# Another order of the columns inside the TensorE matmuls of a short-convolution block

## The chip, the cores and the metric

The kernel runs on one core of one Trainium2 chip. The metric is the device time of one execution in microseconds (us), from runs of the whole program. A profile is one execution recorded by the hardware profiler, and its span runs from the first to the last instruction on the core.

## The reference

With `DEPTH = 1` the reference has one layer, the gated short convolution; the SSD mixer is in the file and isn't reached. `x` has 1024 rows of 1024 numbers, all float32:

```python
def short_conv_mixer(u, w_in, conv_w, w_out):
    z, bg, cg, v = jnp.split(u @ w_in.astype(u.dtype), 4, axis=-1)   # w_in: 1024 x 8192
    y = bg * causal_dwconv(cg * v, conv_w) * jax.nn.silu(z)          # conv_w: 3 x 2048
    return y @ w_out.astype(u.dtype)                                 # w_out: 2048 x 1024

u = rms_norm(x, pre_norm)
out = x + rms_norm(short_conv_mixer(u, w_in, conv_w, w_out), post_norm)
```

Nearly all of the work is in the two matrix products: 1024 x 1024 by 1024 x 8192, then 1024 x 2048 by 2048 x 1024.

## The kernel before

**The products.** Each of the two products is cut into 2 x 2 blocks and done by a scheme with seven block products in place of eight, named a to g; from pair 4 on some of the seven (b, then f, then g) are cut a second time in the same way, into a' to g'. A number is kept as the sum of two parts, hi and lo, of type float32r, and a product is three matmuls: lo by hi, hi by lo, hi by hi. A matmul here multiplies a stationary tile of 128 x 128 (weights, loaded by an instruction of its own that the profile calls LDWEIGHTS) by a moving tile of 128 rows, and adds the result to a tile of PSUM, one bank of 512 float32 a partition. A product of the first level moves 512 columns, a product of the second level 256.

**Five functions issue these matmuls.** `product` (line 865) does the blocks a to g of the input product, 12 matmuls of 512 columns each; `plain` (1117) does the first pair of column blocks, 512 columns, without the scheme of seven; `deep_product` (1460) does a' to g', 6 matmuls of 256 columns each; `out_mm` (1887) does a, c, d, e and g of the output product, 512 columns; `small_mm` (1980) does its b and f, 256 columns. In every one the moving operand and the PSUM tile are walked from the first column to the last. The moving operand is a part of one of the `u` tiles in SBUF (four blocks of 512 columns for hi, four for lo), or of a smaller tile of the second level (`ub..`, `uf..`, `ug.._deep`). The stationary operands are pages of 512 columns (`wah`, `dwb0l` and so on), of which a matmul takes 128.

**Order of the work.** From `plan.record()` on, no instruction is issued at once: `Plan.call` (line 290) writes down each one with the operands it reads and writes, an estimate of its duration, and what it needs. For a view of a tile it takes the lowest and the highest element number, and the count of elements (lines 302 to 330); a matmul is estimated at `n / 2400 + 0.0135` us for `n` elements a partition. `Plan.arrange` (428) then orders the instructions of VectorE, ScalarE, GpSimd and of the DMA queues by due times that come from the order of the matmuls, which is fixed by the list `slots` (1676), and `Plan.emit` (658) issues them. Views are objects of the class `View`, whose `rearrange` keeps both the element numbers and the step to be repeated on the real operand.

**Around the products.** ScalarE copies a page to its hi part, VectorE subtracts to get the lo part, GpSimd builds the sums of blocks that the scheme of seven needs, VectorE and ScalarE take finished banks out of PSUM, and VectorE does the convolution. SBUF places are chosen by hand: tables of page numbers (`HEAD_SLOTS`, line 24; `LOW_PAGES`, 209), of `u` tiles (`U_LAYOUT`, 205), and unused stretches of 64 and 416 bytes between pools. By these tables every matmul operand starts at a multiple of 64 bytes in its partition.

Of the kernel before, what the change touches and what calls it, by code (L numbers as in the profile page):

```python
# [668 lines left out]
def kernel(  # L669
# [16 lines left out]
    nc = plan = Plan(tc.nc)  # L686
# [6 lines left out]
    HB = 512  # L693
# [22 lines left out]
    def bank(name):  # L716
        return psum.tile([P, HB], F32, tag="bank", name=name)
# [136 lines left out]
    UH, UL = {}, {}  # L854
# [7 lines left out]

    banks = {}

    def product(p, i, ks=None):

        w = wt[p, i]
        which = {"b": "y", "e": "v", "f": "v"}.get(i, "x")
        first = i in "abe"
        if first and (p, which) not in banks:  # L870
            banks[p, which] = bank(f"p{which}_{p}")
        ps = banks[p, which]
        for k in range(KH) if ks is None else ks:
            hi, lo = (h[:, k * P : (k + 1) * P] for h in w)
            last = k == KH - 1
            nc.tensor.matmul(ps, lo, UH[i][:, k], start=first and k == 0, stop=False, skip_group_check=True)
            nc.tensor.matmul(ps, hi, UL[i][:, k], start=False, stop=False, skip_group_check=True)
            nc.tensor.matmul(ps, hi, UH[i][:, k], start=False, stop=last, skip_group_check=True)

    sn, cvs = {}, {}  # L880

# [235 lines left out]
    def plain(p, n, half, part, kks=range(4), first=None, last=None):  # L1117

        i = "abef"[2 * half + part]
        if (p, n, half) not in banks:  # L1120
            banks[p, n, half] = bank(f"pp_{p}_{n}_{half}")
        ps, w = banks[p, n, half], plain_w[p, n, part]
        first = part == 0 if first is None else first
        last = part == 1 if last is None else last
        for j, kk in enumerate(kks):
            hi, lo = (h[:, kk * P : (kk + 1) * P] for h in w)
            end = last and j == len(kks) - 1
            nc.tensor.matmul(ps, hi, UH[i][:, kk], start=first and j == 0, stop=False, skip_group_check=True)
            nc.tensor.matmul(ps, lo, UH[i][:, kk], start=False, stop=False, skip_group_check=True)
            nc.tensor.matmul(ps, hi, UL[i][:, kk], start=False, stop=end, skip_group_check=True)  # L1130

    def plain_snap(p, n):
        t = page(f"sp{n}_{p}")
# [69 lines left out]
    for k in range(KH):  # L1203
        plain(0, 0, 0, 0, [k], first=k == 0)
        for t in range(TH - 2 if k < KH - 1 else 0, TH):
            turn(k + KH, t)
# [5 lines left out]
    square_v(TH + 1)  # L1212
    plain_snap(0, 0)
    plain(0, 1, 0, 0)
    for k in (6, 7):
        read_k(k)
    high_plain(0, 1, [1])
    low_plain(0, 1, [1])
    plain_snap(0, 1)
    plain(0, 0, 0, 1)  # L1220
    plain(0, 1, 0, 1)
    rebuild([0])
# [45 lines left out]
    def plain_late(kk, part):  # L1268

        for n in (0, 1):  # L1270
            plain(0, n, 1, part, [kk], first=part == 1 and kk == 0, last=part == 0 and kk == KH - 1)

    product(1, "b", (0, 1))
    turn2(0)
    second(0)
    product(1, "b", (2, 3))
    sn[1, "a"] = page("sna_1")
    nc.scalar.copy(sn[1, "a"], banks[1, "y"])
    product(1, "a", (0, 1))
    turn2(1)  # L1280
    second(1)
# [105 lines left out]
    HH, KQ = HB // 2, KH // 2  # L1387
# [72 lines left out]
    def deep_product(z, c, i):  # L1460


        n, off = DEEP_W[i]
        if z == "f" and i in ("b'", "g'"):
            ps, first = banks[2 * c + (i == "g'"), "v"], False
        elif z == "g" and i in ("b'", "f'", "g'"):
            ps, first = banks[2 * c + (i == "g'"), "x"][:, HH if i == "f'" else 0 :], False
        else:
            which, first = z + DEEP_C[i][0], i in ("a'", "b'", "e'")
            if first:  # L1470
                banks[c, which] = bank(f"p{which[1]}2{z}_{c}")
            ps = banks[c, which]
        ps = ps[:, :HH]
        for k in range(KQ):
            hi, lo = (h[:, off + k * P : off + (k + 1) * P] for h in deep_w[z, c, n])
            if (z, i) in deep:
                uh, ul = (t[:, k] for t in deep[z, i])
            else:
                kk, l0 = {"a'": (k, 0), "b'": (k + KQ, 0), "e'": (k, HH), "f'": (k + KQ, HH)}[i]
                uh, ul = (u[z][:, kk, l0 : l0 + HH] for u in (UH, UL))  # L1480
            nc.tensor.matmul(ps, lo, uh, start=first and k == 0, stop=False, skip_group_check=True)
            nc.tensor.matmul(ps, hi, ul, start=False, stop=False, skip_group_check=True)
            nc.tensor.matmul(ps, hi, uh, start=False, stop=k == KQ - 1, skip_group_check=True)

    def deep_after(c, i):
        which, row, half = DEEP_C[i]
# [190 lines left out]
    for p in range(2, len(PAIRS)):  # L1677
        q, c = p + 1, p // 2
# [91 lines left out]
    for n, slot in enumerate(slots):  # L1770
        if slot[2:]:
            z, i, c = slot
# [24 lines left out]
        i, p = slot  # L1797
# [89 lines left out]
    def out_mm(i, h, q):  # L1887
        which = "v" if i == "e" else "x"
        if (which, q) not in ob:
            ob[which, q] = bank(f"po_{which}{q}")  # L1890
        ps, u, y = ob[which, q], OP["u", i, h], OP["y", i, h]
        for k in range(CQ):
            hi, lo = (y[:, z, k, q * P : (q + 1) * P] for z in (0, 1))
            first, last = i in "abe" and h == 0 and k == 0, h == 1 and k == CQ - 1
            nc.tensor.matmul(ps, lo, u[:, 0, k], start=first, stop=False, skip_group_check=True)
            nc.tensor.matmul(ps, hi, u[:, 1, k], start=False, stop=False, skip_group_check=True)
            nc.tensor.matmul(ps, hi, u[:, 0, k], start=False, stop=last, skip_group_check=True)

    def halves_of(t):
        q = t % TH  # L1900
# [79 lines left out]
    def small_mm(of_, i):  # L1980
        which = {"b'": "y'", "e'": "v'", "f'": "v'"}.get(i, "x'")
        first = i in ("a'", "b'", "e'")
        if first:
            ob[which] = bank(f"p{of_}_{which[0]}")
        if i in OUT_A:
            n, a0 = OUT_A[i]
            yh, yl = (small_op[of_, n][:, z, :, a0 : a0 + HH] for z in (0, 1))
        else:
            yh, yl = (small_op[of_, "X"][:, 0, z] for z in (0, 1))
        if i in OUT_B:  # L1990
            n, b0 = OUT_B[i]
            uh, ul = (small_op[of_, n][:, z, :, b0 : b0 + HH] for z in (0, 1))
        else:
            uh, ul = (small_op[of_, "X"][:, 1, z] for z in (0, 1))
        for j in (0, 1):
            ps = ob[which][:, j * HH : (j + 1) * HH]
            for k in range(CQ):
                hi, lo = (y[:, k, j * P : (j + 1) * P] for y in (yh, yl))

                start, stop = first and j == 0 and k == 0, k == CQ - 1  # L2000
                nc.tensor.matmul(ps, lo, uh[:, k], start=start, stop=False, skip_group_check=True)
                nc.tensor.matmul(ps, hi, ul[:, k], start=False, stop=False, skip_group_check=True)
                nc.tensor.matmul(ps, hi, uh[:, k], start=False, stop=stop, skip_group_check=True)

    def small_add(of_, i):
        which, row, half = DEEP_C[i]
# [5 lines left out]
    def product_b():  # L2012
        for i in SMALL:
            small_mm("b", i)
            small_add("b", i)
            if i == "b'":
                sums_y("b", "f", nc.vector)
                split_small("b", "X")
            elif i in ("e'", "d'", "f'", "g'"):
                split_unit()  # L2020
                fetch_unit()
            if i in ("f'", "g'"):
                for q in (0, 1) if i == "f'" else (2, 3):
                    early_half(q)

    def product_f():
        split_small("f", "B3")
        load_res(0)
        load_res(1)
        for i in SMALL:  # L2030
            small_mm("f", i)
            small_add("f", i)
            if i == "b'":
                split_small("f", "X")
            elif i in ("e'", "d'", "f'", "g'"):
                split_unit()
                if i != "e'":
                    fetch_unit()
            if i in ("f'", "g'"):
                for q in (0, 1) if i == "f'" else (2, 3):  # L2040
                    norm_square(q, 1)
# [33 lines left out]
    for i, h in OUT[:-2]:  # L2075
        if i in "bf":
            if h == 0:
                product_b() if i == "b" else product_f()
            continue
        for q in range(TH):  # L2080
            out_mm(i, h, q)
        BESIDE[i, h]()
        if h == 1:
            for q in range(TH):
                combine(i, q)
# [5 lines left out]
    for q in range(TH):  # L2091
        for h in (0, 1):
            out_mm("g", h, q)
        if q == TH - 1:
            plan.flush(PLAN)
        combine("g", q)
        finish_row(q + TH)
# [24 lines left out]
```

## Time and profile before

| | |
|---|---|
| time, median of 3 runs | 770.9 us (770.83 to 771.6) |
| span of the profiled execution | 768.7 us |
| the profiled execution's own time | not given apart from its span; the median stands 2.2 us above the span |
| matmuls on TensorE | 4320 records: 2244 of 512 columns, 1974 of 256, 102 small ones |
| TensorE busy with matmuls | 758.4 us, 99% |
| VectorE, GpSimd, ScalarE busy | 678.9, 464.1 and 459.4 us |

The counts of 512 and 256 columns follow from the code: a to g and the first pair give 2244, the second level 42 for each of 14 + 13 + 12 blocks and 168 for each of the two small output products, 1974 in all.

How to read the views: all instructions of the kernel carry line 292, the helper that issues them, so they are told apart by tile names. PE is the matmul row of TensorE, PEld its weight loads, DVE is VectorE, ACT ScalarE, POOL GpSimd. In a group's row `px<-u_a,wah` is output, moving operand, weights; the two numbers at the end are busy time and the mean duration of one. Matmuls are pipelined, so a duration is longer than the distance from one start to the next; the chain of waits gives that distance, since each of its pieces runs from the first start of a group to the first start of the next, with the count of instructions behind it.

### The profile page before, as it was taken

The page shows a single profiled execution, that of the slowest core. Times are in us where ns is not written, and L with a number is a line of the kernel's source. Part 1 is how long each engine was busy: PE and PEld are TensorE (multiplying, and loading weights), DVE is VectorE, ACT ScalarE, POOL GpSimd, SP SyncE. Part 2 cuts the span into 40 slices and gives each one's busy share as a digit, 9 for nine tenths or more (in the row PEclk, how much of TensorE's full clock was granted, in tenths as well). Part 3 has the DMA queues.
Part 4 walks back from the last instruction along what each step waited for, and adds up shares of the span by engine and source line. Part 5 has one row for each costly group of instructions (what it writes and reads, how often), then busy time and mean ns, then how long its engine had stood idle before and what let it go on. Part 6 is the DMA issues. An engine that isn't in the chain of part 4 may idle for free.

```text
span 768.7 us, 12791 instructions
## 1 busy us (share of the span) xinstructions
PE 758.4 (99%) x4320; PEld 665.9 (87%) x4320; DVE 678.9 (88%) x1022; ACT 459.4 (60%) x880; POOL 464.1 (60%) x416
## 2 busy tenths in 40 slices
PE   8999999999999999999999999999999999999996
PEld 6888888898989898988898898989888889889885
DVE  6899978999988979989999999898988898877993
ACT  7765678675656565556555665556553656564731
POOL 2509997889675778696789678584739100600421
PEclk9999999999999999999999999999999999999999
DMA  9213325243333547576859484928465998666842
GB/s 317 68 55 84 110 83 150 103 139 130 98 117 97 171 110 200 136 187 164 252 125 255 103 240 97 255 85 211 122 177 179 334 363 291 203 221 204 278 148 109
DMA packets 117137, 130.11 MB, mean 169 GB/s; under 512 B 7320, under 2 KB 74704, under 8 KB 116944
## 3 DMA queue, kind: packets, MB, share of 16 engines
q1 hardware_dynamic: 112560, 120.77, 49.3%
q0 software_dynamic: 4352, 8.39, 7.2%
q8 instruction: 34, 0.56, 0.3%
q14 instruction: 31, 0.25, 0.1%
q10 hardware_dynamic: 160, 0.14, 0.1%
HBM read 101.74 MB, written 44.30 MB: 190 GB/s over the span
## 4 chain that ended last, share of the span: by engine, by line
PE 97%; DVE 1%; DMA 1%; ACT 0%; POOL 0%; issue 0%; POOLq 0%; ACTq 0%
PE px L292 39%; PE pv L292 15%; PE po_x L292 11%; PE px2b L292 5%; PE px2f L292 4%; PE px2g L292 3%; PE po_v L292 3%; PE pp L292 3%; PE pv2b L292 3%; PE pv2f L292 2%; PE pf_x L292 1%; PE pb_x L292 1%; PE py2b L292 1%; PE py L292 1%; PE pv2g L292 1%; PE pb_v L292 1%
## 5 line engine op out<-in xcount | busy, mean ns | idle before, releaser
L292 PE MATMUL px<-u_a,wah 128*128 128x512 f32 x248 | 76.6, 390 | 0.0
L292 PE MATMUL px<-u_c,wch 128*128 128x512 f32 x248 | 76.5, 390 | 0.0
L292 PE MATMUL px<-u_d,wdh 128*128 128x512 f32 x248 | 76.4, 389 | 0.0
L292 PE MATMUL pv<-u_e,weh 128*128 128x512 f32 x248 | 76.3, 389 | 0.0
L292 ACT COPY beside<-raw 128x512 f32<-128x512 f32 x67 | 39.6, 591 | 31.1 <-DVE wal L292 10.4
L292 DVE SCALAR_TENSOR_TENSOR cv<-gpad,cw,cv 128x1024 f32<-128x1024 f32 x32 | 51.6, 1612 | 3.5 <-ACT cv L292 3.3
L292 PEld LDWEIGHTS px<-u_c,wch 128*128 128x128 f32 x248 | 46.5, 188 | 8.9
L292 PEld LDWEIGHTS px<-u_a,wah 128*128 128x128 f32 x248 | 46.6, 188 | 8.9
L292 PEld LDWEIGHTS pv<-u_e,weh 128*128 128x128 f32 x248 | 46.5, 188 | 8.7
L292 PEld LDWEIGHTS px<-u_d,wdh 128*128 128x128 f32 x248 | 46.6, 188 | 8.6
L292 POOL TENSOR_TENSOR sf<-raw,sc 128x512 f32<-128x512 f32 x30 | 47.2, 1573 | 9.5 <-DVE sc L292 7.1
L292 PE MATMUL px<-u_a,wal 128*128 128x512 f32 x124 | 48.4, 391 | 0.0
L292 PE MATMUL px<-u_c,wcl 128*128 128x512 f32 x124 | 48.4, 391 | 0.0
L292 PE MATMUL px<-u_d,wdl 128*128 128x512 f32 x124 | 48.4, 390 | 0.0
L292 PE MATMUL pv<-u_e,wel 128*128 128x512 f32 x124 | 48.2, 389 | 0.0
L292 POOL TENSOR_TENSOR rs_post<-ve_post,minus_half 128x1 f32<-128x1 f32 x7 | 6.5, 941 | 67.3 <-DVE ve_post L292 67.3
L292 POOL TENSOR_TENSOR sc<-se,raw 128x512 f32<-128x512 f32 x25 | 35.0, 1401 | 19.2 <-DVE se L292 10.2
L292 POOL TENSOR_TENSOR raw<-raw,raw 128x512 f32<-128x512 f32 x31 | 44.6, 1437 | 3.2 <-DVE se L292 2.9
L292 ACT COPY sna<-px 128x512 f32<-128x512 f32 x30 | 17.6, 586 | 45.4 <-PE px L292 45.1
L292 POOL TENSOR_TENSOR se<-raw,raw 128x512 f32<-128x512 f32 x22 | 32.8, 1491 | 18.1 <-DMA raw<-in_sc_w_in 11.3
L292 DVE TENSOR_TENSOR wcl<-sc,wch 128x512 fp32r<-128x512 f32 x31 | 31.7, 1023 | 2.8 <-ACT wch L292 2.8
L292 DVE TENSOR_TENSOR sna<-px2b,sna 128x256 f32<-128x256 f32 x56 | 23.2, 415 | 10.2 <-PE px2b L292 10.2
(486 smaller groups left out, 2637.3 us busy)
## 6 DMA issues: line engine op xcount, KB each, us to landing
raw<-in_sc_w_in SPq DMA_DIRECT2D x128, 256.0 KB, 4.7
y_d<-cv SPq DMA_DIRECT2D x16, 512.0 KB, 2.9
s_d<-s SPq DMA_DIRECT2D x32, 256.0 KB, 4.9
t_d<-in_sc_w_out POOLq DMA_DIRECT2D x16, 512.0 KB, 8.5
tb<-in_sc_w_out SPq DMA_DIRECT2D x16, 256.0 KB, 3.5
t_d<-in_sc_w_out SPq DMA_DIRECT2D x16, 256.0 KB, 4.6
t_d<-t_d SPq DMA_DIRECT2D x16, 256.0 KB, 4.5
s<-y_d SPq DMA_DIRECT2D x16, 256.0 KB, 4.6
```

Source lines behind the costliest of these rows:

```text
L292: getattr(engine, name)(*(self.plain(a) for a in args), **{k: self.plain(a) for k, a in kw.items()})
```

## The change

A function `walk` is added, and the output and the moving operand of every matmul of the five functions go through it. It changes the order in which the columns of the operand are read and the columns of the bank are written; the two are changed in the same way, so that each column of the result lands where it did. With 512 columns the order is columns 0 to 3, 16 to 19, 32 to 35 and so on to 496 to 499; then 4 to 7, 20 to 23 and so on; four such passes of 32 pieces. A piece is 16 bytes and the next one starts 64 bytes behind it. With 256 columns it is 0 to 63, 128 to 191, 64 to 127, 192 to 255: four pieces of 256 bytes. The stationary operand, the number of instructions, the tiles and their places are as before. The matmuls of `stir` and the transposes (`turn`) don't go through `walk`.

```diff
     banks = {}
 
+    def walk(a):
+        if a.shape[-1] == HB:
+            return a.rearrange("p (h c n) -> p c h n", c=4, n=4)
+        return a.rearrange("p (h c n) -> p c h n", h=2, n=64)
+
     def product(p, i, ks=None):
...
-            nc.tensor.matmul(ps, lo, UH[i][:, k], start=first and k == 0, stop=False, skip_group_check=True)
-            nc.tensor.matmul(ps, hi, UL[i][:, k], start=False, stop=False, skip_group_check=True)
-            nc.tensor.matmul(ps, hi, UH[i][:, k], start=False, stop=last, skip_group_check=True)
+            nc.tensor.matmul(walk(ps), lo, walk(UH[i][:, k]), start=first and k == 0, stop=False, skip_group_check=True)
+            nc.tensor.matmul(walk(ps), hi, walk(UL[i][:, k]), start=False, stop=False, skip_group_check=True)
+            nc.tensor.matmul(walk(ps), hi, walk(UH[i][:, k]), start=False, stop=last, skip_group_check=True)
...
# deep_product; plain, out_mm and small_mm are changed in the same way
-            nc.tensor.matmul(ps, lo, uh, start=first and k == 0, stop=False, skip_group_check=True)
-            nc.tensor.matmul(ps, hi, ul, start=False, stop=False, skip_group_check=True)
-            nc.tensor.matmul(ps, hi, uh, start=False, stop=k == KQ - 1, skip_group_check=True)
+            nc.tensor.matmul(walk(ps), lo, walk(uh), start=first and k == 0, stop=False, skip_group_check=True)
+            nc.tensor.matmul(walk(ps), hi, walk(ul), start=False, stop=False, skip_group_check=True)
+            nc.tensor.matmul(walk(ps), hi, walk(uh), start=False, stop=k == KQ - 1, skip_group_check=True)
```

More of the change, by code (lines that the diff above doesn't have):

```diff
@@ L1127, in plain @@
             end = last and j == len(kks) - 1
-            nc.tensor.matmul(ps, hi, UH[i][:, kk], start=first and j == 0, stop=False, skip_group_check=True)
-            nc.tensor.matmul(ps, lo, UH[i][:, kk], start=False, stop=False, skip_group_check=True)
-            nc.tensor.matmul(ps, hi, UL[i][:, kk], start=False, stop=end, skip_group_check=True)
+            nc.tensor.matmul(walk(ps), hi, walk(UH[i][:, kk]), start=first and j == 0, stop=False, skip_group_check=True)
+            nc.tensor.matmul(walk(ps), lo, walk(UH[i][:, kk]), start=False, stop=False, skip_group_check=True)
+            nc.tensor.matmul(walk(ps), hi, walk(UL[i][:, kk]), start=False, stop=end, skip_group_check=True)
     def plain_snap(p, n):
@@ L1894, in out_mm @@
             first, last = i in "abe" and h == 0 and k == 0, h == 1 and k == CQ - 1
-            nc.tensor.matmul(ps, lo, u[:, 0, k], start=first, stop=False, skip_group_check=True)
-            nc.tensor.matmul(ps, hi, u[:, 1, k], start=False, stop=False, skip_group_check=True)
-            nc.tensor.matmul(ps, hi, u[:, 0, k], start=False, stop=last, skip_group_check=True)
+            nc.tensor.matmul(walk(ps), lo, walk(u[:, 0, k]), start=first, stop=False, skip_group_check=True)
+            nc.tensor.matmul(walk(ps), hi, walk(u[:, 1, k]), start=False, stop=False, skip_group_check=True)
+            nc.tensor.matmul(walk(ps), hi, walk(u[:, 0, k]), start=False, stop=last, skip_group_check=True)
     def halves_of(t):
@@ L2000, in small_mm @@
                 start, stop = first and j == 0 and k == 0, k == CQ - 1
-                nc.tensor.matmul(ps, lo, uh[:, k], start=start, stop=False, skip_group_check=True)
-                nc.tensor.matmul(ps, hi, ul[:, k], start=False, stop=False, skip_group_check=True)
-                nc.tensor.matmul(ps, hi, uh[:, k], start=False, stop=stop, skip_group_check=True)
+                nc.tensor.matmul(walk(ps), lo, walk(uh[:, k]), start=start, stop=False, skip_group_check=True)
+                nc.tensor.matmul(walk(ps), hi, walk(ul[:, k]), start=False, stop=False, skip_group_check=True)
+                nc.tensor.matmul(walk(ps), hi, walk(uh[:, k]), start=False, stop=stop, skip_group_check=True)
     def small_add(of_, i):
```

## The prediction

> **What bounds the kernel now.** I read the page's busy times and the chain that ended last first.
>
> ```profile
> span 768.7 us, 12791 instructions
> PE 758.4 (99%) x4320; PEld 665.9 (87%) x4320; DVE 678.9 (88%) x1022; ACT 459.4 (60%) x880; POOL 464.1 (60%) x416
> PEclk9999999999999999999999999999999999999999
> PE 97%; DVE 1%; DMA 1%; ACT 0%; POOL 0%; issue 0%; POOLq 0%; ACTq 0%
> ```
>
> TensorE fills 99% of the span and 97% of the chain, and its granted clock is full throughout. A busy PE is not yet a PE at its peak, so the next view is the list of its own waits.
>
> ```profile
> PE pk L292 <- DVE ve_pre L292: 1.5, 1, 1.5
> PE pw L292 <- DVE idle L292: 1.1, 1, 1.1
> PE pp L292 <- ACT u_a L292: 0.5, 1, 0.5
> PE pk L292 <- DVE xa L292: 0.4, 1, 0.4
> ```
>
> That is 3.5 us in all, in the head. The matmuls follow each other, and the time is their count by the distance from one start to the next. The chain in order of time gives that distance (start, us until the next piece, tile, count). First the middle of the input product, then the output product:
>
> ```profile
> 303.14 2.72 PE pv L292 x12
> 305.86 0.71 PE pv2b L292 x6
> 306.57 0.71 PE pv2f L292 x6
> 307.27 0.71 PE px2b L292 x6
> 307.98 0.71 PE px2f L292 x6
> 308.69 2.72 PE px L292 x12
> ...
> 634.92 2.82 PE pb_x L292 x24
> 637.74 2.86 PE pb_y L292 x24
> ...
> 651.89 2.73 PE pb_x L292 x24
> 654.63 21.79 PE po_x L292 x96
> 676.41 21.90 PE po_v L292 x96
> ...
> 718.13 43.82 PE po_x L292 x192
> ```
>
> Twelve 512-column matmuls take 2.72 us, **226.7 ns each**; the output product has 43.82 / 192 = 228.2. The 24 second-level matmuls from 305.86 to 308.69 take 2.83 us, **117.9 ns each**. Two things matter for the change. First, 512 columns take less than twice the time of 256: 226.7 - 117.9 = 108.8 ns for 256 columns (0.425 ns a column), which leaves 117.9 - 108.8 = **9.1 ns a matmul that doesn't grow with the columns**. Second, the distance isn't a constant of the shape: `pb_y` has 2.86 / 24 = 119.2 ns, `pb_x` at 651.89 has 2.73 / 24 = 113.8, with the same 256 columns, engine and clock. They differ in the tiles that they read and in where those lie. An early stage shows the same of 512 columns:
>
> ```profile
> 62.25 2.80 PE py L292 x12
> 67.79 2.72 PE pv L292 x12
> ```
>
> 2.80 / 12 = 233.3 against 226.7 ns. So some of the non-column time depends on how the addresses of the streams fall against each other, which is what a walk alters. Which streams (moving columns, weights, PSUM) no row says.
>
> **The change part by part.** *Removed, added, moved.* No instruction is removed, added or moved. `Plan.call` takes the lowest and highest element and the count from an operand, all of which a reordering leaves alone, so the order on every engine and queue stays, and no wait is added. The walks are address steps within one instruction, which I cost at nothing for the engine's queue: the weight load that each matmul has anyway runs beside it (below).
>
> *Gain from both sides.* If the walk makes no difference, nothing. At most the 9.1 ns go, plus the 1.5 ns by which the output product is slower. With 480 matmuls of `out_mm`, 2244 - 480 = 1764 others of 512 columns and 1974 of 256: 480 x 10.6 = 5.1 us, 1764 x 9.1 = 16.1, 1974 x 9.1 = 18.0; 39.1 us. A loss is bounded further down.
>
> *512 columns.* No row shows a walk. The rows of one shape spread over 226.7 to 233.3, so where the addresses fall is worth at least 6.6 ns, as much as most of the 9.1. The pieces hop each 4 columns, so the moving stream no longer steps through neighbouring addresses as the weights do. I take two thirds of the upper bound: (5.1 + 16.1) x 2/3 = **14.1 us**, that is about 220.6 ns for 226.7.
>
> *256 columns.* This walk has three jumps that a straight one has not, so I take no more than the trace already shows for a better fall of addresses: from 117.9 to the 113.8 of `pb_x` at 651.89, 4.1 ns x 1974 = **8.1 us**.
>
> The Trainium skill, TensorE: Matmul & The Clock Gate, section Back-to-back issue gap, gives N / 2.4 + 2.5 ns at the full clock, 215.8 and 109.2 ns for the two widths as an estimate by it. The rows here are 10.9 and 8.7 ns above it; if the walks reached it, 1764 x 10.9 + 480 x 12.4 + 1974 x 8.7 = 42.4 us would go, close to the upper bound that the rows gave alone.
>
> *What is late next.* A faster TensorE asks its suppliers for the same work in less time. The windows say who has no room (PE, PEld, DVE, ACT and POOL busy; clock, DMA share, GB/s):
>
> ```profile
> 140.00:180.00 40.00, 40.00 (x242) 35.79 (x242) 38.23 (x55) 26.30 (x50) 35.16 (x32) 1.00 0.34 109
> 180.00:220.00 40.00, 40.00 (x242) 35.83 (x242) 37.82 (x60) 22.56 (x43) 30.67 (x27) 1.00 0.33 103
> 300.00:340.00 40.00, 40.00 (x244) 35.94 (x243) 35.62 (x53) 23.45 (x47) 29.92 (x29) 1.00 0.68 179
> 620.00:660.00 40.00, 40.00 (x259) 36.42 (x258) 37.64 (x66) 26.98 (x54) 6.46 (x6) 1.00 0.90 313
> ```
>
> 22.2 us of 758 is 2.9%, so the work of 40 us comes within 38.8. VectorE has 38.23 there in the fullest window (99%), 37.82 in the next, and 37.64 at 620 with the DMA engines at 0.90, which would go to 0.93. At 35.62 (the middle) there is room. I expect short new waits of TensorE on lo parts (VectorE) in those three windows, some 0.7 us each, and give back **2 us**. Were the full 39 us to go, the 40 us would shrink to 37.9, less than VectorE has at 140, and some 4 us would come back.
>
> *The weight loads* are the other thing that could set the distance at 256 columns.
>
> ```profile
> 302.04 0.19 PEld L292 LDWEIGHTS px2f<-ufch_deep,dwf1h 128*128 128x128 f32 x1
> 302.16 0.19 PEld L292 LDWEIGHTS pv2f<-u_f,dwf1l 128*128 128x128 f32 x1
> ```
>
> One takes 0.19 us and starts 0.12 after the one before, so loads overlap each other and every matmul of 256 columns; whether load or stream sets the 117.9 the trace doesn't say. With 512 columns there is twice the time for a load, so this can't be the whole of the 9.1 ns there.
>
> *Sum.* Against the profiled execution: 768.7 of span - 14.1 - 8.1 + 2 = 748.5 us of span. The median stands 2.2 us above that span, so the time is 748.5 + 2.2, **751 us**.
>
> **Rivals.**
> 1. *Only one width gains.* If the weight loads set the pace of the 256-column matmuls, their walk does nothing: 770.9 - 14.1 + 1 = 758 us. For it: PEld's overlap above. Against it: 113.8 ns in `pb_x` with the same load. If it is the 512-column walk that does nothing, 770.9 - 8.1 + 0.5 = 763.
> 2. *Nearly all of the fixed cost goes*: 770.9 - 39.1 + 4 = 736 us. For it: the spread of the rows of one shape, which shows that most of it is a matter of addresses. Against it: no 256-column row is below 113.8.
> 3. *No change*: the 9.1 ns are the price of starting a matmul, whatever the order of its columns, and the address effect is one of the first column alone: 771 us. The change would then not do what a new order of columns could do. Against it: 226.7 to 233.3 in one shape.
> 4. *Slower: each jump costs the stream something.* Place: the 512-column matmuls, with 127 jumps each against 3 in the others. If a jump costs one column's time, 0.425 ns, that is 127 x 0.425 = 54 ns a matmul, 2244 x 54 = 121.2 us, and 1974 x 3 x 0.425 = 2.5 us: 895 us. At a tenth of that it adds 12.4 us to a kernel that otherwise gains 20.2: a gain is left. It decides from the point where 127 jumps eat the 6.3 ns that I take from a 512-column matmul (14.1 us / 2244), 0.05 ns a jump or an eighth of a column. Nothing in the profile speaks for it or against it, since every matmul there walks straight; the upper price comes from the column row, far off. That each piece keeps 4 neighbours together speaks mildly against it. The Trainium skill says in PSUM — Partial Sum Buffer, section Specifications (TRN2), that PSUM has 8-byte cachelines and "any non-contiguous AP slows matmuls significantly"; by that rule this rival is the forecast, though a piece of 16 bytes fills whole lines of that size. No row here shows it.
>
> **How the numbers follow.** Forecast with its own range of 742 to 757: 0.38. Rival 1 (757 to 769): 0.20. Rival 2 (730 to 742): 0.17. Rival 3: 0.08. Rival 4 and anything else above 772.4: 0.17. A difference under 0.2% (1.5 us) can't be told from no change. Faster 0.75, same 0.08, slower 0.17. The range runs from 732, the lower bound of the gain with nothing given back (770.9 - 39.1), to 772, which takes in rival 3; what is left out is rival 4 and the lower edge of rival 2, about 0.2.
>
> **What would show it.** The chain's pieces: 12 matmuls of 512 columns in about 2.65 us for 2.72, `po_x` x96 in about 21.1 for 21.8, six of 256 in 0.68 for 0.71, 24 in about 2.73. If 512 columns fall and 256 don't, rival 1 holds; if 2.60 and 0.66 are reached, rival 2; if `po_x` x96 grows, rival 4, and the growth over 96 x 127 is the price of a jump. VectorE's share should rise from 88% to about 91% at the same busy time, and the list of PE's waits should get entries on VectorE of a microsecond or two between 140 and 220 and near 620; if these sum to over 8 us, what is late next was priced too low. The forecast is wrong if the distances don't move, or if they move by more than a third and the time doesn't follow.

## The result, and the profile after

The changed kernel takes **763.3 us** (763.0 to 763.9), against 770.9 us for the kernel before: a ratio of 0.9903 with a 95% interval of 0.9889 to 0.9917. The change is faster by 7.5 us. The forecast was a gain of 20 us.

The page of the changed kernel, its busy times, clock and shares of the chain:

```profile
span 762.1 us, 12811 instructions
PE 749.9 (98%) x4320; PEld 661.6 (87%) x4320; DVE 676.5 (89%) x1022; ACT 458.9 (60%) x880; POOL 463.3 (61%) x416
PEclk9999999999999999999999999999999999999999
PE 84%; DVE 8%; DMA 2%; issue 2%; POOL 2%; ACT 1%; SPq 0%; DVEq 0%; POOLq 0%; ACTq 0%
```

TensorE is busy for 8.5 us less than before (758.4 to 749.9), and the span is 6.6 us shorter. So 1.9 us came back as idle time. The other engines have their old busy times. TensorE's share of the chain fell from 97% to 84%, although it still fills 98% of the span: once it waits even briefly for a lo part, the chain is followed back through the engine that made it. The list of TensorE's own waits shows how short these are (total us, times, longest):

```profile
PE px L292 <- DVE u_g L292: 0.8, 1, 0.8
...
PE px2b L292 <- DVE dwb1l L292: 0.5, 1, 0.5
...
PE px L292 <- DVE wdl L292: 0.4, 1, 0.4
PE px L292 <- DVE wcl L292: 0.2, 1, 0.2
```

All four are new, all on VectorE, and they sum to 1.9 us. They stand at 403, 415, 551 and 554 us. VectorE has the room of before and no more, as two of the windows that the prediction named show (PE, PEld, DVE, ACT, POOL busy; clock, DMA share, GB/s):

```profile
140.00:180.00 40.00, 40.00 (x247) 35.86 (x246) 38.02 (x55) 25.96 (x50) 35.16 (x31) 1.00 0.35 109
180.00:220.00 40.00, 40.00 (x247) 35.92 (x246) 38.72 (x61) 21.69 (x41) 31.68 (x28) 1.00 0.37 117
```

247 matmuls start in 40 us where 242 did. The chain in order of time (start, us until the next piece, tile, count), first the middle of the input product, then the output product:

```profile
299.77 2.71 PE pv L292 x12
302.48 0.70 PE pv2b L292 x6
303.18 0.68 PE pv2f L292 x6
303.86 0.68 PE px2b L292 x6
304.54 0.68 PE px2f L292 x6
305.22 2.71 PE px L292 x12
...
608.39 21.29 PE po_x L292 x96
629.67 2.83 PE pb_x L292 x24
632.50 2.88 PE pb_y L292 x24
```

Here the reader would swear that the 256-column walk works and the 512-column walk does next to nothing: twelve matmuls of 512 columns take 2.71 us for 2.72, while the 24 of 256 columns behind them take 2.74 us for 2.83. Only the output product shows a faster 512: its first 96 take 21.29 us, and in the profile before they took 21.91,

```profile
613.01 21.91 PE po_x L292 x96
```

and there the 256 columns of `pb_x` and `pb_y` gain nothing. The reading of the two walks turned out to be the reverse of the cause.

For a full account I took the distance from each matmul's start to the next one's over the whole trace. The mean leaves out distances of 300 ns and more, nearly all of which hold a wait or a small matmul in between; us is the count by the mean:

```
                          count    before: mean ns, us     after: mean ns, us     difference
512, input product         1764        227.6   401.5          225.9   398.5          -3.0
512, output product         480        227.9   109.4          223.7   107.4          -2.0
256, input product         1638        117.8   193.0          114.8   188.0          -5.0
256, output product         336        117.6    39.5          117.8    39.6          +0.1
longer distances, beyond the mean                                                    +2.8
```

These sum to -7.1 us. The small matmuls of the head took 0.5 us more, which leaves the 6.6 us by which the span is shorter.

### The profile page after: what moved, and what is told of

The parts are those of the page before. It is cut to its first block, busy times and chain, and to the rows that moved or that the text cites. A ratio compares the mean times of both kernels' runs of the same rounds, so it can differ in the third digit from the quotient of the medians.

```text
span 762.1 us, 12811 instructions
## 1 busy us (share of the span) xinstructions
PE 749.9 (98%) x4320; PEld 661.6 (87%) x4320; DVE 676.5 (89%) x1022; ACT 458.9 (60%) x880; POOL 463.3 (61%) x416
## 4 chain that ended last, share of the span: by engine, by line
PE 84%; DVE 8%; DMA 2%; issue 2%; POOL 2%; ACT 1%; SPq 0%; DVEq 0%; POOLq 0%; ACTq 0%
PE px L292 32%; PE pv L292 13%; PE po_x L292 11%; PE px2b L292 4%; PE px2f L292 3%; PE pp L292 3%; PE po_v L292 3%; PE px2g L292 2%; PE pv2b L292 2%; PE pv2f L292 2%; PE pf_x L292 1%; PE pb_x L292 1%; PE py L292 1%; PE py2b L292 1%; DVE cv L292 1%
## 5 line engine op out<-in xcount | busy, mean ns | idle before, releaser
L292 DVE SCALAR_TENSOR_TENSOR cv<-gpad,cw,cv 128x1024 f32<-128x1024 f32 x32 | 49.5, 1547 | 3.3 <-ACT cv L292 3.2
L292 POOL TENSOR_TENSOR cv<-cv,sne 128x512 f32<-128x512 f32 x13 | 17.6, 1355 | 22.9 <-DVE cv L292 22.9
```

What stands on the lines that cost most here:

```text
L292: getattr(engine, name)(*(self.plain(a) for a in args), **{k: self.plain(a) for k, a in kw.items()})
```

## The experiments

One quantity is needed throughout: the **distance** of a matmul's two streams, which is the start of the moving operand less the start of the weights, in bytes, modulo 256. Below, a distance without a unit, such as 0, 64 or 192, is this one; a distance in ns is the time from start to start. From the places of the operands it is 0 for 1680 of the 1764 matmuls of 512 columns in the input product and 192 for 1630 of the 1638 of 256 columns there. In the output product it is 0 for 288 and 64 for 192 of the 512-column ones, and 0, 64 or 192 for 144, 72 and 120 of the 256-column ones.

The distances sort the gain of the 512-column matmuls. The 192 of the output product at distance 64 fell from 229.0 to 220.5 ns, 1.6 us in all; the 1968 at distance 0, in both products, only from 227.3 to 225.9.

**One width at a time.** Theory A says that each walk speeds up its own matmuls; theory B that TensorE carries something from one matmul to the next, so that walked 512-column matmuls speed up the 256-column ones that follow.

```diff
@@ e1, in walk(), for 512 columns
-            return a.rearrange("p (h c n) -> p c h n", c=4, n=4)
+            return a
@@ e2, in walk(), for 256 columns
-        return a.rearrange("p (h c n) -> p c h n", h=2, n=64)
+        return a
```

> Only the 256-column matmuls walk; those of 512 columns go straight as before. In the trace of the changed kernel six 256-column matmuls of the input product take 0.68 or 0.70 us for 0.71, so 1638 of them save about 4 us. Theory A (the two walks act apart from each other): 512 columns stay at 2.72 us for twelve, the time falls by 3.5 to 4.5 us, to about 767. Theory B (what a matmul takes depends on the one before it, across the change of width): the 512-column pieces move off 2.72 us although their code is as before, and the 256-column pieces off 0.68 and 0.70.

> Only the 512-column matmuls walk. Theory A: pieces of 2.71 us for twelve in the input product (before 2.72) and 21.3 to 21.6 for 96 in the output product (before 21.8 to 21.9), about 3 us less in all, 768. Theory B: twelve behind straight 256-column matmuls differ from 2.71 by some hundredths of a us, and six 256-column ones from 0.71; the two gains don't add up to the 7.5 us of both.

Measured: e1 771.1 us, ratio 1.000 (0.9991 to 1.0008); e2 763.0 us, ratio 0.989 (0.9875 to 0.9908). The chain of e1, where the 256-column matmuls walk:

```profile
302.99 2.72 PE pv L292 x12
305.71 0.71 PE pv2b L292 x6
306.41 0.71 PE pv2f L292 x6
```

and of e2, where they go straight and only the 512-column ones walk:

```profile
299.48 2.71 PE pv L292 x12
302.19 0.70 PE pv2b L292 x6
302.89 0.68 PE pv2f L292 x6
303.57 0.68 PE px2b L292 x6
```

The six straight matmuls of e2 take 0.68 us; the six walked ones of e1 take 0.71, as they did before. Theory A falls. In this kernel the 256-column walk is worth nothing, and the whole gain, that of the 256-column matmuls too, comes from the walk of the 512-column ones.

**The streams alone.** A kernel of matmuls only, without the rest of the computation, in runs of 48: `s` straight, `w` moving operand and PSUM both walked as in the change, `m` only the moving operand walked, `q` only PSUM. First at distance 0, then at 192. It tells apart what of the walk acts, and whether another engine has a part in it. Theory S says that moving columns and weights are read at the same time and collide, the more the more weights there are; runs with 64 and 32 columns of weights test that.

> Matmuls alone, nothing beside them: 39 runs of 48 matmuls (or 72 in turns of 12 of 512 and 12 of 256 columns), each into a bank of its own, the moving blocks and weight pages of a run as in a product (lo hi, hi lo, hi hi over four blocks). It leaves out the computation: its output is the last bank. Names say the form: s straight, w walk of both operands, m walk of the moving operand alone, q walk of PSUM alone; the last number is the distance of moving block and weight page modulo 128 bytes, 0 or 64; k64 and k32 are weights of 64 and 32 columns; x512_c_n other walks. Theory S (the time above the columns is moving reads and weight reads meeting in SBUF): m takes what w takes and q what s takes, 0 and 64 differ, and k64 and k32 take less than 128 columns of weights (of the 9 ns that don't grow with the columns about half and a quarter). Theory P (it is PSUM's writes): q takes what w takes and m what s takes, 0 and 64 agree, the width of the weights makes no difference. Theory T (start-up behind each change of width): 48 walked 512-column matmuls in a row settle at about 220 ns, and in turns of twelve they average 225 or more. If all that theory S says holds without any other engine at work, contention with DVE, ACT or DMA is no part of it.

The chain of m1, four pieces for 512 columns at distance 0, four for 256 at distance 0, then the same at 192:

```profile
15.80 10.88 PE s L99 x48
26.68 10.74 PE w L99 x48
37.42 10.72 PE m L99 x48
48.14 10.90 PE q L99 x48
59.05 5.75 PE s L99 x48
64.80 5.76 PE w L99 x48
...
82.08 11.20 PE s L99 x48
93.28 10.88 PE w L99 x48
104.16 10.87 PE m L99 x48
115.03 11.20 PE q L99 x48
126.23 5.45 PE s L99 x48
131.68 5.44 PE w L99 x48
```

- With nothing else running, 48 straight matmuls take 10.88 us, 226.7 ns each, the kernel's figure. No other engine is part of it.
- `w` is `m` and `q` is `s`, at both distances. The walk of the moving operand does everything; the 127 jumps in PSUM gain nothing and cost next to nothing (10.90 us for 10.88).
- The 512-column walk gains 3 ns at distance 0 (10.88 to 10.74) and 6.7 ns at 192 (11.20 to 10.88). The kernel has, of these two, the distance at which straight 512-column matmuls are faster.
- The 256-column walk does nothing at either distance. Straight, 256 columns take 113.5 ns at distance 192 and 119.8 at 0. So the kernel's 117.8 at distance 192 was not their own pace.
- Narrower weights: from 128 to 64 and 32 columns a weight load's duration falls from 188 to 134 and 108 ns, but 512 columns go from 226.7 to 229.8 and 231.6 ns, and 256 columns from 113.4 to 118.8 and back to 113.4. That part of theory S fails: the loss does not shrink with the number of weights.
- In turns of twelve, at the kernel's distances of 0 and 192, straight 512-column matmuls take 229 ns and the 256-column ones behind them 117.8, walk or no walk of their own. With walked 512-column ones (224 to 226 ns) the three groups of 256 columns take 114.2, 117.8 and 117.5.

**The distance, and turns of the two widths.** Weights shifted by steps of 16 bytes, 24 matmuls each of straight 512, walked 512 (pieces of 4), straight 256 and walked 256 (here pieces of 4 as well), and then both widths in turns.

> Matmuls alone again (the output is the last bank, nothing else is computed). Runs of 24, straight (s) and walked in pieces of 4 columns with hops of 64 bytes (w), 512 and 256 columns, with the weights shifted against the moving blocks by 0 to 240 bytes in steps of 16; then turns of 12 walked 512-column and 24 straight 256-column matmuls with weights shifted by 0, 64, 128 or 192 bytes for each (mx), three with straight ones (ms). If the distance is moving reads and weight reads meeting in SBUF, it is a function of the shift with a period of 128 or 256 bytes, flat in neither form: straight 512 between 226.7 and 233.3 at shifts of 0 and 64, straight 256 between 113.3 and 120.0, walked 512 between 220 and 227, with its best at one of the shifts of 64 or 192 (the output product of the changed kernel has 220 to 222 where its weights lie 64 bytes off modulo 256, and 223 where they lie at 0). If instead the time is a fixed start of each matmul, all 16 shifts of a form agree within a ns. In turns, if the phase at which 512 columns end decides the pace of the 256-column matmuls behind them, their mean moves between 113.3 and 117.7 with the shift of the 512-column weights though their own stays.

The chain of m2, at shifts of 0, 48, 64 and 192 bytes (a shift of 64 is the distance 192, a shift of 192 the distance 64), in the order just given:

```profile
15.58 5.44 PE s L142 x24
21.02 5.38 PE w L142 x24
26.40 2.88 PE s L142 x24
...
65.36 5.60 PE s L142 x24
70.96 5.28 PE w L142 x24
...
81.79 5.59 PE s L142 x24
87.38 5.55 PE w L142 x24
92.93 2.73 PE s L142 x24
...
198.24 5.53 PE s L142 x24
203.76 5.36 PE w L142 x24
209.12 2.84 PE s L142 x24
```

Straight 512 columns: 226.7 ns at distance 0 (5.44 / 24), 228 to 234 at all others. Walked: 220.0 at a shift of 48 (5.28 / 24), 224.2 at 0, 223.3 at 192, 231.3 at 64. Straight 256: 113.8 at a shift of 64, 120.0 at 0, 118.3 at 192. The distances 64 and 192 differ, so the pattern doesn't repeat after 128 bytes; whether it does after 256 no run shows. The distance modulo 256 isn't the whole setting either: at 192 the walked 512 columns take 231.3 ns here and 226.7 in m1 (10.88 / 48), where the pages lie elsewhere and other runs came before. In turns, with the 512-column matmuls walked at distance 0 and the 256-column ones at 192 as in the kernel, successive groups of 256 columns took 113.7, 117.8 and 117.7 ns with the same operands; with straight 512-column ones 117.8. So the matmuls alone give the kernel's faster 256 columns in one group of three only. With the 512-column ones walked at distance 64 they took 113.3 to 113.8, and the 512-column ones 220.4 to 222.8. That suggested moving the kernel's 512-column streams to distance 64.

**The shift in the kernel.** The upper `u` tiles move by 64 bytes against the pages, once with the walk of 512 columns alone (e3) and once with everything straight (e4). 1516 of the 512-column matmuls of the input product are then at distance 64; 192 of the output product go from 64 to 128.

```diff
 U_LAYOUT = (
-    ((0, 3, 4), 64),
-    ((1, 2, 5, 6), 0),
+    ((0, 3, 4), 128),
+    ((1, 2, 5, 6), 192),
```

> 512-column matmuls walk, 256-column ones go straight, and the four upper u tiles (the moving blocks of a, c, d and e) lie 64 bytes higher against the weight pages, so that moving block and weights of the 512-column matmuls of the input product are 64 bytes apart modulo 256 and not 0; those of the 256-column ones stay 192 apart. In the runs of matmuls alone, turns at these distances took 220.0 to 222.8 ns a 512-column matmul (225 at distance 0) and 113.8 a 256-column one. Theory S (the fall of the two addresses sets the pace): twelve 512-column matmuls take 2.64 to 2.67 us for 2.71, about 1490 of them save some 4 ns, 6 us; e and g of the output product get distance 128 and lose about 0.8 us; 757 to 758 us, if VectorE follows. Rival (suppliers hold TensorE by now): pieces of 2.66 us are there, but PE's waits on VectorE grow by several us and the time stays at 761 to 763. Rival (the gain was not from the addresses): 2.71 us as without the shift.

> The kernel before, every matmul straight, with the same 64 bytes of shift alone. Theory S: straight 512-column matmuls took 228.8 ns at a distance of 64 against 226.7 at 0, and behind 256-column ones more, so twelve take 2.75 to 2.79 us for 2.72, the 256-column ones stay at 117.8; 1490 x 2 to 5 ns, 774 to 778 us. Rival (the layout doesn't matter without the walk): 771 us.

Measured: e3 761.25 us, ratio 0.9874 (0.9857 to 0.9892); e4 776.0 us, ratio 1.0061 (1.0045 to 1.0077). The chain of e3:

```profile
297.41 2.67 PE pv L292 x12
300.08 0.70 PE pv2b L292 x6
300.78 0.68 PE pv2f L292 x6
...
602.88 21.91 PE po_x L292 x96
```

and of e4:

```profile
296.66 2.76 PE px L292 x12
299.43 0.70 PE px2b L292 x6
...
617.35 22.04 PE po_x L292 x96
```

The same 64 bytes make twelve walked matmuls faster (2.71 to 2.67 us) and twelve straight ones slower (2.72 to 2.76): the streams' distance and the order of the columns act together. e4 came out as expected. e3 missed its figure of 757 to 758 us, in part because the output product lost more than I had reckoned: against e2 its 512-column matmuls went from 224.2 ns to 227.7, 1.7 us, and the 256-column ones from 117.8 to 119.3, 0.5 us, against 3.9 us won by the 512-column ones of the input product. The number of the rival, suppliers that hold TensorE, came, but not its sign: the listed waits of TensorE sum to 5.1 us in e3 and 5.2 in e2.

**Another way to the same distance.** In place of the shift, the pages of first-level weights are sought on the low shelf first and all other pages on the high one, with the walk of 512 columns alone.

```diff
-        if name[:2] in ("wb", "wf", "wg"):
-            first = low
-        elif name[0] == "w" or name[:2] == "dw":
-            first = high
-        else:
-            first = slots
+        first = low if name[0] == "w" else high
```

> 512-column matmuls walk, 256-column ones go straight, the u tiles lie as before; instead the weight pages of the first-level blocks are taken from the ten lower pages where one is free, and every other page from the upper ones. By the addresses 1344 of the 1764 512-column matmuls of the input product are then 64 bytes off modulo 256 (352 at 0), and the output product stays as it was (288 at 0, 192 at 64). Theory S: twelve 512-column matmuls 2.67 us where both are at 64, the output product 21.3 to 21.6 for 96 as with the walk alone and not 21.9 as with the shifted tiles; 758 to 760 us. Rival (pages that come back sooner make the copies wait): PE's waits grow and the time is 762 or more.

Measured: 762.7 us, ratio 0.989 (0.9873 to 0.9906). A miss. The 512-column matmuls of the input product fell to 223.7 ns as in e3, but against e3 the 256-column ones of the input product rose from 114.7 to 115.8 ns, 1.9 us (102 of them are now at distance 0), and the distances of 300 ns and more hold 2.4 us more beyond the mean. TensorE's wait for one lo part is longer than in e3 (0.3 us), and no run shows why:

```profile
PE px2b L292 <- DVE dwb1l L292: 1.1, 1, 1.1
```

**Is there a memory?** Turns of 12 walked 512-column matmuls and 12 or 24 straight 256-column ones, with the weights of one width at a fixed shift and those of the other moved by 16 bytes from run to run.

> Matmuls alone (the output is the last bank, nothing else is computed): turns of 12 walked 512-column, 12 straight 256-column, 12 walked 512-column, 24 straight 256-column matmuls, three times. The weights of the 512-column ones are shifted by 0 to 240 bytes in steps of 16 with those of the 256-column ones at 64, then the other way round with the 512-column ones at 192. If the phase at which one width ends decides the pace of the next, the 256-column means move between 113.3 and 117.8 with the shift of the 512-column weights alone, and the walked 512-column ones between 220 and 232. If only a matmul's own two addresses count, the 256-column means of the first 16 runs agree within a ns, and so do the 512-column means of the others.

Mean distances from start to start within a group, with the weights of the 256-column matmuls at a shift of 64 bytes in every run; six of the 16 shifts, lowest to highest group:

```
shift of the 512's weights    512, walked (ns)    256, straight (ns)
   0                          223.8 to 225.8      113.7 to 117.8
  16                          229.4               113.4 to 113.5
  32                          227.5               117.6 to 117.7
  48, from the second turn    235.7               114.0 to 114.7
 176                          224.2               113.3
 192                          222.8               113.8 to 114.5
```

The 256-column matmuls have the same operands in all rows, and yet they take from 113.3 to 117.8 ns, by the addresses of *other* matmuls before them. In the first row even those are the same in every turn, and one group takes 113.7 ns and another 117.8: what counts reaches further back than the group just before. It goes the other way too: walked 512-column matmuls at a shift of 192 take 220.0 to 228.8 ns, by the shift of the 256-column ones. At a shift of 48 the 512-column ones take 220.0 ns alone and 235.7 in turns from the second turn on, so a figure from a run of one width doesn't carry over.

**The change with the shift.** The changed kernel again, and with the two lines of `U_LAYOUT` from e3, on one chip.

> The changed kernel, both walks, with the four upper u tiles 64 bytes higher. If the 256-column walk does nothing here either, this is the walk of 512 columns with the shift: 761.3 us, 1.3% under the kernel before. If the two walks help each other once the 512-column ones stand at a distance of 64, below 759.

> The changed kernel as it is, on the same chip and against the same runs, so that the shift can be judged: 763.3 us, and the shifted one 2 us under it if the shift is a gain beyond the noise.

Measured: with the shift 761.1 us, ratio 0.9870 (0.9857 to 0.9884); without it 763.8, ratio 0.9908 (0.9894 to 0.9922). The shift adds 2.7 us to the change's gain. It is the fastest version that was run, with e3 (the same without the 256-column walk) level with it, and beats both kernels.

## Why the prediction was right and wrong

**What bounds the kernel: right.** The time is the count of matmuls by the distance of their starts. What changed is that distance in time, with 2 to 3 us of new waits: the clock is full as before and the engines have nearly the same busy times.

**The 512-column term, 14.1 us: mis-sized, 5.0 us came** (3.0 + 2.0). The step that failed is "I take two thirds of the upper bound", about 220.6 ns. The 9.1 ns that don't grow with the columns were taken for a matter of addresses, of which the walk would remove most. That pace came where the distance is 64 (220.5 ns for 192 matmuls of the output product); 1968 of the 2244 stand at distance 0, where a walked matmul alone takes 223.3 to 224.2. In the kernel the gain there is smaller still, down to 225.9 ns: the start distances of a typical group of twelve in the input product, behind 256-column ones, run

```
before:  227, 227, 226, 227, 227, 226, ...
after:   229, 227, 226, 237, 225, 218, 230, 224, 221, 218, 230, 224
```

The walked stream of m1 starts in the same way, with 225.2 ns for its first twelve and 223.3 for all later ones, so in groups of twelve part of the loss is the time to get into step. It isn't the whole: the output product has runs of 96 at distance 0, and the one of `po_x` on `oy_c`, 21.64 us,

```profile
649.41 21.64 PE po_x L292 x96
```

has 225.4 ns; single twelves in it reach 223.3, others are at 227.7. The one on `oy_d` averages 226.9. Why these don't stay at 223.3 is open. The prediction read the spread of rows, 226.7 to 233.3, as a sign that 226.7 could be improved as much again. In truth 226.7 was the best straight value over the 16 shifts of m2: the layout already had that part of the gain. The larger gains of a walk are at distances where the straight stream is slower (at a shift of 48 from 233.3 to 220.0).

**The 256-column term, 8.1 us: 5.0 us came, none of it by the step given.** The step that failed is the price of "this walk", taken as a better fall of addresses. That 113.8 ns can be had was right, and the input product nearly reached it (114.8). But e1 has the walk and no gain, and e2 has the gain without the walk. Pieces of 64 columns are 256 bytes, and m1 shows them to be the same as no walk. The 256-column matmuls at distance 192 run at 113.3 by themselves; straight 512-column ones before them hold them at 117.8, and in the kernel walked ones let them go after some five matmuls. That it is the walk of the 512-column ones is shown by e1 and e2; how it acts is not, since the matmuls alone at the same distances had only one group in three at the faster pace. The prediction said rightly that the distance isn't a constant of the shape and sought the reason in the matmul's own tiles; what ran before them was left out. In the output product nothing came: of its 336 matmuls of 256 columns, 216 lie at distances 0 and 64, where straight ones alone take 117.7 to 120, and of the 120 at 192 three groups of 24, `pb_x` at 651.89 among them, had 113.8 to 114.2 already.

**What is late next, 2 us: the size and the engine right, the place wrong.** The new waits are 1.9 us, on lo parts from VectorE, as said; the distances of 300 ns and more grew by 2.8 us. But none is in the three windows that were named, 140 to 220 and 620 to 660 us, so that the size came out is partly luck. Two are at 551 and 554: VectorE was busy for 29.49 of the 30 us from 530 to 560 already before the change, which windows of 40 us hide. The one on `dwb1l` at 403 is no mark of a faster TensorE, since e1, at the old pace, has it too (0.4 us). VectorE's share rose to 89% and not 91%, since TensorE asked for less than forecast.

**The sum.** 768.7 - 5.0 - 5.0 + 0.1 + 2.8 = 761.6, against a measured span of 762.1 (the 0.5 us between them are the small matmuls of the head); in the prediction it was 768.7 - 14.1 - 8.1 + 2. The result lies inside the range of 732 to 772 and outside the forecast's own of 742 to 757.

**Rivals.** Rival 1 had the nearest number, 763 us, for the case that the 512-column walk does nothing. That it was met is luck: the chain of after looks just like it, and the experiments show the opposite. Its other case, with weight loads that set the pace of 256 columns, isn't borne out either: loads shortened from 188 to 108 ns leave 256 columns at 113.3. Rival 2 fails: no walk that was tried had the 9.1 ns, and the best run of 512 columns at any distance is 6.7 ns under the straight one at distance 0 (220.0 for 226.7). Rival 3 fails by e2. Rival 4, a price on each jump, fails at this size of piece and hop: with 127 jumps in PSUM alone a matmul takes 10.90 / 48 = 227.1 ns for 226.7. It isn't far off at others: in m1 the same 127 jumps in both operands take 246.6 ns with hops of 128 bytes and 275.9 with 256, that is 0.16 and 0.39 ns a jump, near the upper price of 0.425. The Trainium skill's rule in PSUM — Partial Sum Buffer, section Specifications (TRN2), that any non-contiguous pattern slows matmuls significantly, is contradicted here for a walk of PSUM alone in pieces of 16 bytes, 64 bytes apart.

**What stays open.** The runs show that the pace depends on the distance modulo 256 or more, on the order of the moving columns and on what ran before. They don't show what it is in TensorE or in SBUF that has this memory, nor why narrower weights don't help. Nor do the matmuls alone account for the kernel's figures at distance 0 and 192 (225.9 and 114.8 ns). A walk of the 256 columns in pieces of 4 was not tried in the kernel; alone, in m2, it takes 115.7 ns for 119.8 at distance 0, where 144 of the output product stand.

## What to carry to other kernels

The pace in a row of the profile need not be a property of that row alone: before crediting an edit with it, undo the edit in one shape at a time, since here the row that got faster was one whose own edit did nothing. The places of the two operands against each other and the order of the moving columns were one setting here and had to be tried together: the same 64 bytes cost 5 us straight and gained 2.7 us walked. Measure such a setting in the kernel's own sequence of shapes, as the best of a stream alone (220.0 ns) was among the worst in turns (235.7).

## What the runs showed of the hardware that was not expected

- Memory from matmul to matmul: 113.3 to 117.8 ns for the same 256 columns, by the addresses of the 512-column matmuls that ran before them.
- About half of the runs of one kind in m1 and m2 have a mean distance within 0.3 ns of a multiple of 3.33: 113.33, 120.0, 220.0, 223.33, 226.67, 233.33. Others, such as 231.3, don't. No run says why.
- The size of the piece and of its hop matter. Other walks of 512 columns at distance 0 in m1, each of both operands: pieces of 16 bytes with a hop of 32 bytes 233.4 ns, 64 bytes 223.8, 128 bytes 246.6, 256 bytes 275.9; pieces of 32 bytes 230 to 233; pieces of 256 bytes and more 227 to 228. Pieces of 8 bytes (hop 32, moving operand and PSUM) take 461 ns, twice the time. The Trainium skill says in SBUF — State Buffer, section Specifications (TRN2), that a 16-byte line needs at least two hits for the full bandwidth; pieces of 8 bytes give it two, and they are the slow ones here. Since PSUM was walked in the same pieces, no run shows which of the two memories makes them slow.
- The lowest mean distance of a run of 512 columns is 220.0 ns. By the Trainium skill, TensorE: Matmul & The Clock Gate, section Back-to-back issue gap, it would be 215.8, an estimate from the formula that the page gives for an isolated matmul. No run here reached that.
